# Half of an output projection as one pair group with two Strassen steps, its last eight K tiles taken token half by token half

## The chip, the cores and the metric

One core of a Trainium2 chip runs the whole program. The metric is device time in microseconds (us) of one execution; the median of several runs stands for a kernel. The engines are named as the profile names them: PE multiplies matrices, DVE and ACT work element by element, POOL does little here, SP issues the loads, and DMA engines move the data.

## The reference, cut to what matters

The program is one layer of an encoder over 256 tokens of width 2048, in float32. The change is in the first feed-forward block, just before the first layer norm:

```python
D_MODEL, SEQ, D_FF = 2048, 256, 5504

def swiglu_ffn(x, w_in, w_out):
    g, u = jnp.split(x @ w_in, 2, axis=-1)
    return (jax.nn.silu(g) * u) @ w_out

h = x
h = layer_norm(ALPHA * h + 0.5 * swiglu_ffn(h, ffn1_w_in[l], ffn1_w_out[l]), ln_ffn1_g[l], ln_ffn1_b[l])
mix = hybrid_mixer(h, w_in[l], gate_bias[l], rel_bias[l], q_a_norm[l], w_q_b[l], kv_a_norm[l],
                   w_kv_b[l], w_o_a[l], w_o_b[l], w_out[l], cos, sin)
```

The mixer's first product in the kernel is `h @ w_va` (a part of `w_in`). A second, equal feed-forward block (`ffn2`) ends the layer.

## The kernel before, in words

**Arithmetic.** Every float32 operand is split into a high part (rounded to the fast matmul format, by ACT) and a low part (the rest, by DVE). A product takes three matmuls: high by high, high by low, low by high. A *K tile* is 128 rows of the contraction; a matmul multiplies one K tile of 128 tokens with 512 columns of weights. The 256 tokens are two *token halves* (`tt` 0 and 1), whose residual rows are the tiles `h0` and `h1`.

**Weights.** `run` walks a list of items; each names the weight pieces it needs. `fetch` loads a piece (128x2048, 1 MB) into one of three `raw` tiles over SP's queue, ACT casts it into a high tile and DVE subtracts for the low tile (`halves`). High and low go to a pair of the pools `hi`/`lo` (two pairs), or to named blocks (`T0` to `T3`, `X0` to `X3`, `H0` to `H5`) where the item gives tags. The tile framework puts each engine's instructions in one fixed order by priorities and its own estimate of readiness; on the chip each engine works through its order and waits where an input is missing.

**Pair groups.** `pair_group` computes 1024 columns for both token halves in four PSUM tiles (bank of 512 columns each), two K tiles to a step: a plain step is `mm_pair`, 24 matmuls. A step in `at` goes through Strassen's scheme (`mm_sums`): the 2x2 block product of two K tiles and two column halves takes seven block products in place of eight, 21 matmuls. Its price: `weight_sums` forms four sums of weight blocks on DVE, these are cast and subtracted as well, four sums of the activations ("forms", `forms_step`) must exist, and four more PSUM tiles are filled, which `shared` combines once per group (two ACT copies, four DVE operations) before `then` adds the results to `h0` and `h1`.

**The place of the change.** The hidden width (43 K tiles) is worked in two parts, 24 and 19 K tiles. For the second part of `ffn1` the hidden tiles are the blocks `H0` to `H4` (four K tiles in each, three in `H4`). Columns 0 to 1023 are a pair group with Strassen steps 3, 5 and 7 (`out_pair`). Columns 1024 to 2047 (quarters n = 2 and 3 of 512 columns) are done by `out_proj`: quarter 2 in five pieces of four K tiles (the last has three), each for both token halves; of quarter 3 the first piece likewise; its last four pieces go through `skewed`, which runs token half 0 through all four and then token half 1 through the same weights, kept in the `T` and `X` blocks. Every finished PSUM tile is added to `h0` or `h1` (`finish`), and `ln_piece` takes statistics of the quarter.

**The hand-over to the layer norm.** `skewed` weaves the norm of token half 0 into the work of token half 1: `ln_scale` (aggregate the statistics, nine small DVE operations for the reciprocal root `y` and the offset `nb`), then `ln_T`: scale a quarter of `h0` (DVE and ACT alternately), transpose it on PE, apply gain and bias on the way out of PSUM (ACT and DVE alternately, 128 columns each), and split it into the tiles `T0` to `T3`. The next product, `h @ w_va`, starts with token half 0 and reads `T0` first.

Of the kernel before, what the change touches and what calls it, by code (L numbers as in the profile page):

```python
# [28 lines left out]
AT_FIRST = 4, 6  # L29
SUMS_OUT = ({3: ("X1", 0), 5: ("X1", 1), 7: ("X0", 0), 9: ("X0", 1)},  # L30
            {3: ("X1", 0), 5: ("X1", 1), 7: ("X0", 0)})
SUMS_GATE, AT_GATE = {**SUMS_IN, 5: ("F", 0)}, ((2, 4, 5, 6), (2, 4, 5, 6), (2, 4, 6), (2, 4, 6))
ORDER_GATE = (0, 2, 1, 4, 5, 3, 6, 7)
SUMS_YB = {4: ("T0", 0), 6: ("T0", 1), 2: None}
# [67 lines left out]
class Kernel:  # L102
# [451 lines left out]
    def ffn(self, tag, xT, st, first=None, steps=None, late=None, before=None, tags=None):  # L554


        t = self.t
        f0 = bank = 0
        turn = None
        fx = {}  # L560
        for half, nf in enumerate(F_SPLIT):
            hid, fh, homes = Act([]), {}, SUMS_OUT[half]
            end = half == len(F_SPLIT) - 1
            form = lambda c, fh=fh, homes=homes, hid=hid: self.forms_step(fh, homes, c, lambda: hid)
            for g in range(-(-nf // 4)):
# [12 lines left out]
                if turn and n < 4:  # L578
                    turn[5] = turn.pop(6)
                self.weave(main, turn or {}, prio=0)  # L580
                for c, (home, _) in homes.items():
                    if home == "X1" and c // 2 == g - 1:
                        self.add(form(c))
                hidden, turn = self.hidden(ps, bank, g, n, hid, qs)
                self.add(hidden, prio=SOON)
                if before and 2 <= j < 6:
                    self.add(lambda q=j - 2: self.gb_apply(2, self.h, (q,)), prio=LATE)
                if j == 0 and first is not None:
                    for c in set(SUMS_IN) - set(AT_FIRST):
                        self.add(self.forms_step(fx, SUMS_IN, c, xT, False))  # L590
                bank ^= 1
            if end and late:
                self.add(lambda: setattr(self, "cut", True))

            def out(hid=hid):
                x = lambda: hid
                src = [t[tag + "_w_out"][g, :, f0 * 1024:(f0 + nf) * 1024] for g in range(2)]
                self.out_pair(bank, src[0], 0, nf, x, homes, fh, half == 0, st if end else None,
                              SUM_HOME + ("H5",) if end else SUM_HOME)
                if end:  # L600
                    self.out_proj(tag + "_w_out_r", nf, x, False, st, steps, tags, 2, cut=tags is None)
# [41 lines left out]
    def group_tiles(self, j):  # L643
        return {(tt, g): self.group_tile(j) for tt in range(2) for g in range(2)}

    def pair_group(self, bank, src, n, nk, x, at, fx, ps, qs, then=None, sums_in=SUM_HOME, order=None):


        order = range(-(-nk // 2)) if order is None else order
        sums = [c for c in order if c in at]  # L650
        for i, c in enumerate(order):
            kts = range(2 * c, min(2 * c + 2, nk))
            ap = src[:, kts[0] * 2 * n:(kts[-1] + 1) * 2 * n]
            if c in at:
                close = i + 1 < len(order) and order[i + 1] in at

                def fn(w, c=c, close=close):
                    if c == sums[0]:
                        qs.update((a, self.group_tile(bank + 1)) for a in range(4))
                    self.mm_sums(ps, qs, w, n, x(), fx[c], 2 * c, c == sums[0], c == sums[-1], close)  # L660
                self.add(fn, Sums(ap, *sums_in))
                if c == sums[-1]:
                    self.add(lambda: self.shared(qs, n), prio=SOON)
                    if then:
                        self.add(then)
                continue

            def fn(w, i=i, kts=kts):
                if i == 0:
                    ps.update(self.group_tiles(bank))  # L670
                self.mm_pair(ps, w, n, x(), kts, i == 0, i == len(order) - 1)
            self.add(fn, ap)

    def shared(self, qs, n):
# [85 lines left out]
    def out_proj(self, wname, nk, x, scale, st, steps=None, tags=None, n0=0, other=False, cut=False):  # L760
# [48 lines left out]
                part(n, (0, 1), i, ps)  # L809
        if steps is not None:  # L810
            self.skewed(lambda tt, j, **kw: part(3, (tt,), last + j, ps, **kw), steps(0), tags)

    def skewed(self, part, steps, tags=None):

# [874 lines left out]
def _halves(w):  # L1689

    w = w.reshape(w.shape[0], -1, 2, 512)
    return [w[:, :, i].reshape(w.shape[0], -1) for i in (0, 1)]


def _cols(v):
    return v.reshape(-1, P).T


def _layout(i):
# [8 lines left out]
    for f in ("ffn1", "ffn2"):  # L1708
        w = a[f + "_w_in"][0]
        r[f + "_w_in"] = _pairs(  # L1710
            w[:, D_FF:D_FF + NG * 512], w[:, :NG * 512], 512, [AT_FIRST] + [SUMS_IN] * (NG - 1))
        r[f + "_w_in_r"] = _pairs(
            w[:, D_FF + NG * 512:], w[:, NG * 512:D_FF], D_FF - NG * 512, [SUMS_IN])
        w = a[f + "_w_out"][0]
        at = [*SUMS_OUT[0], *(F_SPLIT[0] // 2 + c for c in SUMS_OUT[1])]
        r[f + "_w_out"] = _pairs(*_halves(w), 512, [at, at])
        r[f + "_w_out_r"] = _tok(w[F_SPLIT[0] * P:, D // 2:])
    r["ffn2_gate"] = _tok(a["ffn2_w_in"][0][:, :512])
    r["ffn2_up"] = _tok(a["ffn2_w_in"][0][:, D_FF:D_FF + 512])
    w = a["w_in"][0]  # L1720
# [56 lines left out]
```

## Time and profile before

| what | us |
|---|---|
| median of 3 runs | 2434.72 (2433.43 to 2435.46) |
| the profiled execution | 2432.52 |
| its span in the profile | 2430.7 |
| PE busy | 2422.3 |
| DVE busy | 2130.9 |
| ACT busy | 1553.2 |
| the 19 K tiles of columns 1024 to 2047, first to last matmul of it | 630.5 to 683.4 |

The profile names a line by its number in this kernel and a tile by the program's name without its buffer number. "A<-B,C" means that A is written from B and C. A timeline row gives start, length, engine, line, operation, tiles, shape and count, and in brackets how long the engine was idle before it and who ended the wait. Busy PE time is modelled, since matmuls are pipelined: one matmul is given as about 0.39 us, but the next starts 0.227 us later.

### The profile page before, as it was taken

Reading aid. Unit: us, or ns where it says so; the run is one execution under the profiler, and the core shown is the slowest. Engines: PE = TensorE matmul, PEld = TensorE weight load, DVE = VectorE, ACT = ScalarE, POOL = GpSimd, SP = SyncE. Lnnn points to the kernel's source line nnn. Section 1 sums busy time; section 2 is a strip of 40 time slices with the busy share of each in tenths; the row PEclk is TensorE's granted clock in tenths of the full one; section 3 lists DMA queues with packets and bytes.
Section 4 is the critical chain, followed back from the end, with each engine's and each line's share of the span. In section 5 each row is a group of like instructions: output and inputs, shape, how many; then the busy total and the mean of one; then the engine's idle time right before and its main releaser. Section 6 shows DMA issues by size and latency. Waiting matters only on the chain.

```text
span 2430.7 us, 29702 instructions
## 1 busy us (share of the span) xinstructions
PE 2422.3 (100%) x11280; PEld 2022.8 (83%) x11280; DVE 2130.9 (88%) x2437; ACT 1553.2 (64%) x2022; POOL 35.9 (1%) x81
## 2 busy tenths in 40 slices
PE   9999999999999999999999999999999999999999
PEld 8888888888888888888888888888888888888887
DVE  8999989899889998779788889979879999888997
ACT  6676745666555557878565687765666675556662
POOL 0000000000000001000000000000000000000000
PEclk9999999999999999999999999999999999999999
DMA  7766656667656657776577577655556766666665
GB/s 268 252 212 214 207 200 222 210 201 219 224 176 215 216 195 248 229 210 176 183 246 256 167 241 213 220 181 192 190 199 214 229 221 210 220 207 207 200 220 182
DMA packets 176414, 516.20 MB, mean 212 GB/s; under 512 B 111728, under 2 KB 112496, under 8 KB 121104
## 3 DMA queue, kind: packets, MB, share of 16 engines
q1 hardware_dynamic: 170816, 495.83, 61.6%
q0 software_dynamic: 4592, 17.30, 2.2%
q8 instruction: 88, 1.44, 0.2%
q10 hardware_dynamic: 864, 1.18, 0.1%
q14 instruction: 54, 0.44, 0.1%
HBM read 485.30 MB, written 2.10 MB: 201 GB/s over the span
## 4 chain that ended last, share of the span: by engine, by line
PE 89%; DVE 4%; ACT 3%; DMA 1%; issue 1%; SPq 0%; DVEq 0%; ACTq 0%
PE at L311 24%; PE mm L311 23%; PE at L366 11%; PE mm L366 11%; PE mm L298 10%; PE mm L277 4%; PE mm L279 2%; DVE lo L267 2%; ACT hi L264 1%; PE at L1034 1%; PE at L1505 0%; PE at L277 0%; DMA raw<-w_xv 0%; PE at L1088 0%; ACT H L854 0%
## 5 line engine op out<-in xcount | busy, mean ns | idle before, releaser
L264 ACT CAST hi<-raw 128x1024 fp32r<-128x1024 f32 (+1 forms) x852 | 804.0, 981 | 458.0 <-PE at L311 150.1
L267 DVE TENSOR_TENSOR lo<-raw,hi 128x2048 fp32r<-128x2048 f32 (+1 forms) x427 | 902.0, 2114 | 134.8 <-ACT hi L264 129.0
L311 PE MATMUL mm<-hi,T 128*128 128x512 f32 (+1 forms) x1312 | 307.5, 384 | 0.8 <-DVE v L400 0.7
L311 PEld LDWEIGHTS mm<-hi,T 128*128 128x128 f32 x1312 | 244.5, 188 | 46.9 <-DVE v L400 1.1
L264 ACT CAST X<-H 128x1024 fp32r<-128x1024 f32 (+1 forms) x170 | 174.8, 1035 | 160.9 <-DVE H L248 119.9
L311 PE MATMUL at<-hi,T 128*128 128x512 f32 x1136 | 272.3, 390 | 0.0
L311 PEld LDWEIGHTS at<-hi,T 128*128 128x128 f32 x1136 | 213.3, 188 | 44.5
L267 DVE TENSOR_TENSOR X<-H,X 128x2048 fp32r<-128x2048 f32 (+1 forms) x85 | 191.4, 2252 | 64.7 <-ACT X L264 64.7
L311 PE MATMUL mm<-lo,T 128*128 128x512 f32 (+1 forms) x656 | 158.4, 383 | 0.0
L311 PE MATMUL at<-lo,T 128*128 128x512 f32 x568 | 141.0, 389 | 0.0
L311 PEld LDWEIGHTS mm<-lo,T 128*128 128x128 f32 x656 | 122.3, 188 | 22.4
L311 PE MATMUL at<-hi,H 128*128 128x512 f32 x560 | 133.8, 390 | 0.0
L311 PEld LDWEIGHTS at<-lo,T 128*128 128x128 f32 x568 | 106.7, 188 | 22.1
L311 PEld LDWEIGHTS at<-hi,H 128*128 128x128 f32 x560 | 105.0, 188 | 21.5
L250 DVE TENSOR_TENSOR H<-H,raw 128x512 f32<-128x512 f32 (+1 forms) x170 | 115.4, 679 | 2.2
L311 PE MATMUL mm<-hi,H 128*128 128x512 f32 x480 | 115.5, 392 | 0.1
L311 PEld LDWEIGHTS mm<-hi,H 128*128 128x128 f32 x480 | 89.6, 188 | 18.9 <-DVE w L684 0.5
L248 DVE TENSOR_TENSOR H<-raw 128x1024 f32<-128x1024 f32 (+1 forms) x85 | 102.1, 1201 | 0.6 <-DMA raw<-w_gate 0.4
L366 PE MATMUL mm<-X,X 128*128 128x512 f32 x342 | 91.4, 393 | 0.0
L264 ACT CAST X<-raw 128x1024 fp32r<-128x1024 f32 (+1 forms) x54 | 55.4, 1035 | 47.9 <-DVE raw L250 38.6
L366 PE MATMUL at<-X,X 128*128 128x512 f32 (+1 forms) x315 | 82.6, 386 | 0.7 <-ACT X L264 0.7
L854 ACT COPY w<-w 128x1024 uint16<-128x1024 uint16 (+1 forms) x60 | 75.7, 1275 | 1.4 <-DMA w<-w 1.4
(387 smaller groups left out, 4151.3 us busy)
## 6 DMA issues: line engine op xcount, KB each, us to landing
raw<-ffn_w_in SPq DMA_DIRECT2D x150, 1024.0 KB, 4.9
raw<-ffn_w_out SPq DMA_DIRECT2D x66, 1024.0 KB, 4.9
raw<-w_gate SPq DMA_DIRECT2D x32, 1024.0 KB, 4.8
raw<-ffn_w_out_r SPq DMA_DIRECT2D x16, 1024.0 KB, 4.9
raw<-w_qk SPq DMA_DIRECT2D x16, 1024.0 KB, 5.6
raw<-w_o_b SPq DMA_DIRECT2D x16, 1024.0 KB, 4.8
raw<-w_out SPq DMA_DIRECT2D x16, 1024.0 KB, 5.0
raw<-w_xk SPq DMA_DIRECT2D x16, 1024.0 KB, 5.4
```

Source lines behind the costliest of these rows:

```text
L248: self.nc.vector.tensor_tensor(two[0], two[1], raw[:, :m].unsqueeze(1).to_broadcast([P, 2, m]), ALU.add)
L250: self.nc.vector.tensor_tensor(t[:, a * m:a * m + m], t[:, b * m:b * m + m], raw[:, a * m:a * m + m], ALU.add)
L264: self.last_hi = self.nc.scalar.copy(hi[:, c:d], src[:, c:d])
L267: self.last_lo = self.nc.vector.tensor_tensor(lo[:, :n], src, hi[:, :n].bitcast(F32), ALU.subtract)
L277: self.nc.tensor.matmul(ps, hi[j], x.both(kt), start=(j == 0), stop=False)
L279: self.last_mm = self.nc.tensor.matmul(ps[:, :S], lo[j], x.at(0, kt), start=False, stop=(j == n - 1))
L298: self.last_mm = self.nc.tensor.matmul(ps, x.at(xi, kt)[:, tt * P:(tt + 1) * P], w[wi][:, j * 512 + c:j * 512 + c + m], start=(start and j ...
L311: self.last_mm = self.nc.tensor.matmul(ps[tt, g][:, :n], x.at(xi, kt)[:, tt * P:(tt + 1) * P], w[wi][:, c:c + n], start=first and j + wi + ...
L366: self.last_mm = self.nc.tensor.matmul(bank[:, :m], a[xi], v[wi][:, c * m:(c + 1) * m], start=own and first and wi + xi == 0, stop=own and ...
L854: self.nc.scalar.copy(self.words(u, n).rearrange("p (c k) -> p k c", k=2), self.words(s, n).rearrange("p (k c) -> p k c", k=2))
L1034: nc.tensor.matmul(ps[:, c0:c0 + nk], q[:, tt * P:(tt + 1) * P], k[:, :nk], start=(j == 0), stop=(j == len(parts) - 1))
```

## The change

For `ffn1` alone, columns 1024 to 2047 of the second part become one pair group over all four PSUM tiles, left open at its end (`open_end`), followed by `skewed`:

- The pair group takes the steps 6, 3, 8, 5, 7, 9 (two K tiles each, step 9 only K tile 18). Steps 3 and 5 go through Strassen's scheme, with the activation sums that the first 1024 columns used already (block `X1`), and weight sums in `H5`, `X2` and `X3`.
- The remaining eight K tiles (0 to 5, 8 and 9) are four pieces of 128x2048: for quarter 2 two pieces, for quarter 3 two. Token half 0 takes all four, then token half 1 the same four. Each of the four PSUM tiles is finished when its second piece is done.
- The weights are laid out anew to fit. The loads keep their number (ten) and bytes (9.5 MB).

`ffn2` keeps `out_proj`. The diff, cut to its core:

```diff
+AT_OUT, OUT_ORDER, OUT_ENDS = (3, 5), (6, 3, 8, 5, 7, 9), (0, 1, 2, 3, 4, 5, 8, 9)
...
-                if end:
+                if end and tags:
+                    self.out_skew(bank ^ 1, src[1], tag + "_w_out_r", nf, OUT_ORDER, OUT_ENDS, x,
+                                  {c: homes[c] for c in AT_OUT}, fh, False, st, steps, tags, SUM_HOME + ("H5",))
+                elif end:
                     self.out_proj(tag + "_w_out_r", nf, x, False, st, steps, tags, 2, cut=tags is None)
...
-                self.mm_pair(ps, w, n, x(), kts, i == 0, i == len(order) - 1)
+                self.mm_pair(ps, w, n, x(), kts, i == 0, not open_end and i == len(order) - 1)
...
+    def out_skew(self, bank, src, wname, nk, order, ends, x, at, fx, scale, st, steps, tags=None, sums_in=SUM_HOME):
+        nc, t, h = self.nc, self.t, self.h
+        ps, qs, kept = {}, {}, {}
+        def shared():
+            for (tt, a), s in qs["add"].items():
+                hs = h[tt][:, (2 + a) * 512:(3 + a) * 512]
...
+                    nc.vector.tensor_tensor(hs, hs, s, ALU.add)
+        def part(tt, j, tags=None, held=0, keep=False, again=False):
+            a, i = divmod(j, 2)
+            grp = ends[4 * i:4 * i + 4]
+            def fn(w=None):
+                if keep:
+                    kept[j] = w
+                w = kept.pop(j) if again else w
+                n, p = 2 + a, ps[tt, a]
+                self.mm_tok(p, tt, w, x(), grp, False, i == 1)
+                if i:
+                    with self.prio(SOON):
+                        self.finish(tt, n, p, False, st)
+            ap = t[wname][a, :, 2048 * i:2048 * i + 2048]
+            self.add(fn, *(() if again else ((ap, tags),)), held=held)
+        self.pair_group(bank, src, 512, nk, x, at, fx, ps, qs, shared, sums_in, order, True)
+        self.skewed(part, steps(0), tags)
```

Outside this stage every engine keeps its order. Three places inside it are shown; a number in a name marks the one buffer.

On DVE, at the end of the stage, before: the last steps for the root `y`, the offset `nb`, the scaling of `h0`, the first four pieces out of PSUM, the low half of `T0`, and then the last sum of token half 1 (`mm_756`).

```order
L379 TENSOR_SCALAR y_765_5091<-a_766_5092,y_765_5091 128x1
L403 SCALAR_TENSOR_TENSOR nb_767_5094<-mv_763_5089,y_765_5091 128x1
L413 TENSOR_SCALAR h0_101<-h0_101,mv_763_5089,y_765_5091 128x512 x2
L430 TENSOR_SCALAR w2_773_5150<-at_772_5145,vecs_89 128x128
L430 TENSOR_SCALAR w2_775_5163<-at_774_5158,vecs_89 128x128
L430 TENSOR_SCALAR w2_773_5150<-at_772_5145,vecs_89 128x128
L430 TENSOR_SCALAR w2_775_5163<-at_774_5158,vecs_89 128x128
L256 TENSOR_TENSOR T0_768_5140<-w2_773_5150,T0_768_5140 128x4x128
L754 TENSOR_TENSOR h1_102<-h1_102,mm_756_5015 128x512
```

The same place with the change (lines count one to four higher; `mm_732` is token half 1 of quarter 3, the last PSUM tile of the stage):

```order
L379 TENSOR_SCALAR a_780_5116<-y_779_5115,v_778_5114 128x1
L758 TENSOR_TENSOR h1_102<-h1_102,mm_732_4831 128x512
L380 TENSOR_SCALAR y_779_5115<-a_780_5116,y_779_5115 128x1
L391 BN_STATS bn_728_4824<-h1_102 128x6
L379 TENSOR_SCALAR a_780_5116<-y_779_5115,v_778_5114 128x1
L396 BN_AGGR mv_794_5236<-bn_728_4824 128x2
L380 TENSOR_SCALAR y_779_5115<-a_780_5116,y_779_5115 128x1
L401 TENSOR_SCALAR v_795_5237<-mv_794_5236 128x1
L404 SCALAR_TENSOR_TENSOR nb_781_5118<-mv_777_5113,y_779_5115 128x1
L414 TENSOR_SCALAR h0_101<-h0_101,mv_777_5113,y_779_5115 128x512 x2
```

The sum of the stage's last PSUM tile has moved from behind `T0` to a place ahead of `nb`, the scaling of `h0` and `T0`.

On PE, the transposes of `h0` (tiles `at`) and the first product of `w_va`, before:

```order
L298 MATMUL mm_756_5015<-X1_748_4962,H3_655_4336 128x512 x4
L421 MATMUL at_772_5145<-ident_90,h0_101 128x128 x4
L421 MATMUL at_774_5158<-ident_90,h0_101 128x128 x4
L298 MATMUL mm_756_5015<-X2_750_4968,H4_707_4680 128x512 x6
L298 MATMUL mm_756_5015<-X3_751_4969,H4_707_4680 128x512 x3
L421 MATMUL at_776_5182<-ident_90,h0_101 128x128 x4
L421 MATMUL at_778_5195<-ident_90,h0_101 128x128 x4
L298 MATMUL mm_788_5229<-hi_753_4997,T0_768_5140 128x512 x8
```

With the change:

```order
L299 MATMUL mm_732_4831<-X3_767_5000,H1_561_3742 128x512 x2
L299 MATMUL mm_732_4831<-X3_767_5000,H2_610_4055 128x512 x2
L422 MATMUL at_786_5171<-ident_90,h0_101 128x128 x4
L422 MATMUL at_788_5184<-ident_90,h0_101 128x128 x2
L422 MATMUL at_790_5211<-ident_90,h0_101 128x128
L422 MATMUL at_788_5184<-ident_90,h0_101 128x128
L422 MATMUL at_790_5211<-ident_90,h0_101 128x128
L422 MATMUL at_788_5184<-ident_90,h0_101 128x128
L422 MATMUL at_790_5211<-ident_90,h0_101 128x128 x2
L422 MATMUL at_792_5224<-ident_90,h0_101 128x128 x4
L299 MATMUL mm_802_5258<-hi_769_5030,T0_782_5166 128x512 x8
```

All 16 transposes now stand behind the last matmul of token half 1, where the first eight stood nine matmuls ahead of it; the first matmul of `w_va` follows them at once, as before.

On ACT, from the scaling of `h0` to the high half of `T0`, before:

```order
L415 ACTIVATE h0_101<-h0_101,nb_767_5094,y_765_5091 128x512 x2
L428 ACTIVATE w2_773_5150<-at_772_5145,vecs_89 128x128
L428 ACTIVATE w2_775_5163<-at_774_5158,vecs_89 128x128
L428 ACTIVATE w2_773_5150<-at_772_5145,vecs_89 128x128
L428 ACTIVATE w2_775_5163<-at_774_5158,vecs_89 128x128
L255 CAST T0_768_5140<-w2_773_5150 128x4x128
```

With the change:

```order
L416 ACTIVATE h0_101<-h0_101,nb_781_5118,y_779_5115 128x512 x2
L429 ACTIVATE w2_787_5176<-at_786_5171,vecs_89 128x128
L429 ACTIVATE w2_789_5189<-at_788_5184,vecs_89 128x128
L429 ACTIVATE w2_791_5216<-at_790_5211,vecs_89 128x128
L429 ACTIVATE w2_787_5176<-at_786_5171,vecs_89 128x128
L429 ACTIVATE w2_789_5189<-at_788_5184,vecs_89 128x128
L429 ACTIVATE w2_791_5216<-at_790_5211,vecs_89 128x128
L429 ACTIVATE w2_793_5229<-at_792_5224,vecs_89 128x128
L256 CAST T0_782_5166<-w2_787_5176 128x4x128
```

Seven pieces out of PSUM stand ahead of the cast of `T0`, where there were four.

More of the change, by code (lines that the diff above doesn't have):

```diff
@@ L644, in group_tiles, with pair_group @@
         return {(tt, g): self.group_tile(j) for tt in range(2) for g in range(2)}
-    def pair_group(self, bank, src, n, nk, x, at, fx, ps, qs, then=None, sums_in=SUM_HOME, order=None):
+    def pair_group(self, bank, src, n, nk, x, at, fx, ps, qs, then=None, sums_in=SUM_HOME, order=None, open_end=False):
         order = range(-(-nk // 2)) if order is None else order
@@ L811, in out_proj @@
             self.skewed(lambda tt, j, **kw: part(3, (tt,), last + j, ps, **kw), steps(0), tags)
+    def out_skew(self, bank, src, wname, nk, order, ends, x, at, fx, scale, st, steps, tags=None, sums_in=SUM_HOME):
[4 more added lines that the diff above has]
+                hs = h[tt][:, (2 + a) * 512:(3 + a) * 512]
+                if scale:
+                    nc.vector.scalar_tensor_tensor(hs, hs, ALPHA, s, ALU.mult, ALU.add)
+                else:
+                    nc.vector.tensor_tensor(hs, hs, s, ALU.add)
[15 more added lines that the diff above has]
+        self.skewed(part, steps(0), tags)
     def skewed(self, part, steps, tags=None):
@@ L1692, in _halves, with _tiles @@
     return [w[:, :, i].reshape(w.shape[0], -1) for i in (0, 1)]
+def _tiles(w, kts):
+    import numpy as np
+    return np.concatenate([w[k * P:k * P + P] for k in kts])
 def _cols(v):
@@ L1715, in _layout @@
         at = [*SUMS_OUT[0], *(F_SPLIT[0] // 2 + c for c in SUMS_OUT[1])]
-        r[f + "_w_out"] = _pairs(*_halves(w), 512, [at, at])
-        r[f + "_w_out_r"] = _tok(w[F_SPLIT[0] * P:, D // 2:])
+        skew = f == "ffn1"
+        at2 = [*SUMS_OUT[0], *(F_SPLIT[0] // 2 + c for c in AT_OUT)] if skew else at
+        r[f + "_w_out"] = _pairs(*_halves(w), 512, [at, at2])
+        w = w[F_SPLIT[0] * P:, D // 2:]
+        r[f + "_w_out_r"] = _tok(_tiles(w, OUT_ENDS) if skew else w)
     r["ffn2_gate"] = _tok(a["ffn2_w_in"][0][:, :512])
```

## The prediction

> **What bounds the kernel now.** I read the page first, then the timelines of PE, DVE and ACT around 620 to 700 us, then a table by stretches.
>
> ```profile
> PE 2422.3 (100%) x11280; PEld 2022.8 (83%) x11280; DVE 2130.9 (88%) x2437; ACT 1553.2 (64%) x2022; POOL 35.9 (1%) x81
> PE 89%; DVE 4%; ACT 3%; DMA 1%; issue 1%; SPq 0%; DVEq 0%; ACTq 0%
> core 0: us, PE busy (x) PEld busy (x) DVE busy (x) ACT busy (x) POOL busy (x), PEclk, DMA share, GB/s
> 628.30:680.10 51.80, 51.80 (x230) 42.74 (x228) 39.33 (x40) 23.40 (x25) 0.00 (x0) 1.00 0.72 248
> ```
>
> PE is busy for the whole span and carries 89% of the chain of waits. So a matmul less saves its interval, and any new idle time of PE is added in full, since nothing later on PE can give it back. In the stretch that is changed DVE works 39.3 of 51.8 us. Now PE there, by start and length:
>
> ```profile
> 630.49 1.98 PE L298 MATMUL mm<-hi,H 128*128 128x512 f32 x8
> 667.21 4.92 PE L298 MATMUL mm<-X,H 128*128 128x512 f32 x21
> 671.97 5.60 PE L298 MATMUL mm<-T,H 128*128 128x512 f32 x24
> 677.41 2.88 PE L298 MATMUL mm<-X,H 128*128 128x512 f32 x12
> 680.27 1.06 PE L421 MATMUL at<-ident,h 128*128 128x128 f32 x8
> 681.09 2.32 PE L298 MATMUL mm<-X,H 128*128 128x512 f32 x9
> 683.25 1.03 PE L421 MATMUL at<-ident,h 128*128 128x128 f32 x8
> 684.04 2.28 PE L298 MATMUL mm<-hi,T 128*128 128x512 f32 x8
> ```
>
> 21 matmuls from 667.21 to 671.97 are 0.2267 us each. PE is without a gap but for 677.41 + 12 x 0.2267 = 680.13 to 680.27. What hides the layer norm of token half 0 is token half 1: from 671.97 on, PE has 36 matmuls before the first transposes and nine more before the rest. DVE and ACT meanwhile:
>
> ```profile
> 628.34 2.29 DVE L267 TENSOR_TENSOR lo<-raw,hi 128x2048 fp32r<-128x2048 f32 x1
> 674.40 0.69 DVE L390 BATCH_NORM_STATS2 bn<-h 128x6 f32<-128x512 f32 x1
> 677.20 0.26 DVE L395 BATCH_NORM_AGGREGATE mv<-bn 128x2 f32<-128x24 f32 x1
> 679.55 0.16 DVE L403 SCALAR_TENSOR_TENSOR nb<-mv,y 128x1 f32<-128x1 f32 x1
> 679.63 1.00 DVE L413 TENSOR_SCALAR h<-h,mv,y 128x512 f32<-128x512 f32 x2
> 683.68 0.69 DVE L256 TENSOR_TENSOR T<-w,T 128x512 fp32r<-128x512 f32 x1 [0.34 <-ACT T L255]
> 684.29 0.68 DVE L754 TENSOR_TENSOR h<-h,mm 128x512 f32<-128x512 f32 x1
> 679.75 1.52 ACT L415 ACTIVATE h<-h,nb,y 128x512 f32<-128x512 f32 x2 [4.88 <-DVE nb L403]
> 681.17 1.73 ACT L428 ACTIVATE w<-at,vecs 128x128 f32<-128x128 f32 x4
> 683.03 1.14 ACT L255 CAST T<-w 128x512 fp32r<-128x512 f32 x2
> ```
>
> The low half of `T0` starts at 683.68 and PE takes up `w_va` at 684.04; only at 684.29 does DVE add the last sum of token half 1. That order is what the change turns round.
>
> **Matmuls.** Before, 19 K tiles x 2 token halves x 2 quarters x 3 passes = 228. Now two steps of 24 become 21: 222. Saved: 6 x 0.2267 = 1.36 us. From 630.49 the last one is issued out at 630.49 + 222 x 0.2267 = 680.8.
>
> **DVE's added work** in the stage, by the costs of one operation:
>
> ```profile
> L267 DVE TENSOR_TENSOR lo<-raw,hi 128x2048 fp32r<-128x2048 f32 x16 | 36.5, 2287 | 7.7 <-ACT hi L264 7.7
> L267 DVE TENSOR_TENSOR lo<-raw,hi 128x1024 fp32r<-128x1024 f32 x1 | 1.2, 1220 | 0.0
> L250 DVE TENSOR_TENSOR H<-H,raw 128x512 f32<-128x512 f32 x6 | 4.1, 686 | 0.0
> L248 DVE TENSOR_TENSOR H<-raw 128x1024 f32<-128x1024 f32 x3 | 3.7, 1218 | 0.0
> L631 DVE TENSOR_TENSOR h<-h,w 128x512 f32<-128x512 f32 x4 | 2.6, 685 | 0.0
> L681 DVE TENSOR_TENSOR w<-w,mm 128x512 f32<-128x512 f32 x1 | 0.7, 681 | 0.0
> ```
>
> Weight sums, 2 x (1.22 + 2 x 0.69) = 5.2; low parts, one more 2048 and one 1024, 2.29 + 1.22 = 3.5; four operations of `shared` and four sums into `h`, 8 x 0.68 = 5.5. Together 14.2, and about 13 with the 0.08 by which queued operations overlap (16 of them). ACT gets three more casts of 1024 (1.0 each, the second row below) and two copies beside 23.4 us of work in 51.8, so ACT has room. DVE up to the last sum of token half 1: 39.3, less the norm chain from 677.20 (2.9), plus 13, plus the aggregation and five small operations of the root, which now stand ahead of that sum (1.3) = 50.7, of the 52.5 us from 628.34 to 680.8. So DVE, which before waited 12.5 us in this stretch, can wait less than 2 now before it comes late. What it waits for are casts, and they for loads:
>
> ```profile
> raw<-ffn_w_out_r SPq DMA_DIRECT2D x16, 1024.0 KB, 4.9
> 655.98 2.00 ACT L264 CAST T<-raw 128x1024 fp32r<-128x1024 f32 x2 [2.03 <-DMA raw<-ffn_w_out_r]
> ```
>
> Number, bytes and queue of the loads stay, but a load is issued when DVE frees a `raw` tile, so a late DVE also makes late loads. `X1`, `X2` and `X3` serve the Strassen steps until step 5 is through and can be refilled only then, some 50 matmuls (11 us) before PE reads `X1` and `X2`; casts of 2.0 and a subtraction of 2.3 must fit in there, and a load of 4.9 where its `raw` tile comes free late. I take 0.5 us of lateness, bounds 0 and 2.
>
> **First stall, at the hand-over.** The sum of `mm_732` stands on DVE ahead of the rest of `h0`'s root. It waits for the stage's very last matmul; behind it wait `nb`, the scaling of `h0`, so the transposes, so `T0`, so all of PE. From PE's last matmul: how soon does DVE take up such a sum?
>
> ```profile
> 2416.09 5.04 PE L298 MATMUL mm<-X,H 128*128 128x512 f32 x30
> 2421.17 0.42 DVE L787 TENSOR_TENSOR h<-h,mm 128x256 f32<-128x256 f32 x1
> ```
>
> 0.04 after the modelled end, and that end is 0.39 - 0.23 = 0.16 behind the interval: 0.2. Then the sum 0.6 and the statistics 0.6 (0.68 and 0.69 less overlap), six small operations at 0.16 (the `nb` row) to 0.24 (677.20 to 679.63 over ten), so 1.0 to 1.45, half of the scaling row 0.5, and 0.1 until PE starts. Together 3.0 to 3.5; I take 3.25.
>
> **Second stall.** The 16 transposes take about 1.65 (681.09 - 680.27 is 0.82 for eight); they existed before and cost nothing new. But `w_va` needs `T0`: from `nb`, ACT scales two quarters (681.17 - 679.75 = 1.4), then seven pieces at 1.73 / 4 = 0.43 make 3.0, then the cast 0.6: 5.0. PE, from `nb`: 0.65 to the transposes, 1.65 for them, 2.3. It waits 2.7. One matmul later it needs the low half, 0.69 behind the cast: 0.5 more. So 3.2; with pieces at 0.35 it is 2.6, with DVE late on its own seven pieces 3.7.
>
> **Sum.** -1.36 (matmuls) - 0.14 (the gap at 680.13) + 0.5 + 3.25 + 3.2 = +5.45 us. Nothing hides it: PE has no other work queued there. The norm of token half 1 gains: its statistics are now taken earlier, and its transposes come after 36 matmuls (8 us), as before. The profiled execution (2432.52) becomes 2438.0, the median of the runs (2434.72), which lies 2.2 above it, 2440.2. The ends are -1.5 + 0 + 3.0 + 2.6 = +4.1 and -1.5 + 2 + 3.5 + 3.7 = +7.7: 2438.8 to 2442.4.
>
> **Rivals.** First, **PE's clock falls** in the hand-over, and the next matmuls run slowly. The rows on it:
>
> ```profile
> 1.06 4.21 PE L493 MATMUL at<-w 128*128 128x128 f32 x18 [1.06 <-DVE w L470]
> 5.04 4.84 PE L311 MATMUL mm<-hi,T 128*128 128x512 f32 x16
> 2425.26 1.02 PE L1617 MATMUL mm<-T,w 128*128 128x512 f32 x2
> 2427.00:2429.00 2.00, 0.00 (x0) 0.00 (x0) 0.66 (x2) 0.00 (x0) 0.00 (x0) 1.00 0.97 349
> 2429.00:2430.70 1.70, 0.00 (x0) 0.00 (x0) 0.00 (x0) 0.00 (x0) 0.00 (x0) 0.52 0.16 52
> ```
>
> PE's last matmul ends at 2426.28; the granted clock (the figure ahead of the DMA share) is 1.00 until 2429.0 and 0.52 behind: it halved after some 2.8 us without work. The stalls here are about 3.2 and 3.2 us with 1.65 of transposes between them. At half clock a matmul takes 0.23 longer; at the program's start, with work from 1.06 on, the 16 from 5.04 still took 4.84 - 0.16 = 4.68, 1.05 more than 16 x 0.2267, part of it perhaps waiting for data. So a fall costs between 1.05 and half of some 5 us, 2.5; I take 1.8: 2442.0. Against it: transposes are work too, and no row shows how little suffices. The Trainium skill ("TensorE: Matmul & The Clock Gate", Part 1 and Part 4) has a free-running window of about 3.4 us, half clock after an idle one, and says that transposes don't count as busy in the same way; the end of this trace agrees with the first, no run here shows the second. By that rule alone an estimate would be 1.7 us for each cold window.
>
> Second, **the hand-over is short**, the case on the other side. If pieces leave PSUM at 0.35 or faster, DVE is never late and the small operations take 0.16, the terms are 0, 3.0 and 2.6: +4.1, 2438.8, which can't be told from no change. It decides from 6.4 us of stalls downwards. For it: PE's stalls are paced by short operations whose waits overlap. Against it: DVE's room of 1 to 2 us.
>
> Third, **only the matmuls count**: the hand-over is hidden as before, and the time is 2434.72 - 1.36 = 2433.4. For it: before, PE waited nowhere here. Against it stands the order on DVE. The six matmuls themselves are gone by count, so the saving is not in doubt.
>
> Fourth, **the group starves**: `X1` to `X3` come late and PE waits inside the group, 2 us or more on top: 2442.2 and higher.
>
> **Chances.** Forecast 0.47, falling clock 0.24, short hand-over 0.20, matmuls only 0.03, starved group 0.06. 0.2% (4.9 us, about what a measurement of this kernel tells from no change) is at 2439.6, so some 0.1 of the forecast's 0.47 counts as no change. Slower: 0.37 + 0.24 + 0.06 = 0.67; within 0.2%: 0.10 + 0.20 + 0.02 = 0.32; faster 0.01. The range must take in the short hand-over and the falling clock: 2437.3 to 2443.8.
>
> **What would show it.** In the changed profile: 222 matmuls in the stage; PE idle about 3.2 us ahead of the first transposes of `h0`, put down to DVE, and 2.5 to 3.5 more ahead of the first `w_va` matmuls, put down to ACT and DVE; DVE's sum of `mm_732` within 1 us of PE's last matmul. A lower clock would show in a table of stretches behind it. I am wrong if PE goes through the hand-over with less than 4 us of idle time, if it waits over 2 us inside the group, or if the time moves elsewhere.

## The result, and the profile after

| | us |
|---|---|
| median before | 2434.72 (2433.43 to 2435.72, 7 runs) |
| median after | 2441.22 (2440.6 to 2443.9, 7 runs) |
| ratio | 1.0032, 95% interval 1.0022 to 1.0041 |
| predicted | 2440.2 (2437.3 to 2443.8) |

The changed kernel is slower by 6.5 us. Its profiled execution is the longest of the seven (2443.9), so its hand-over may be longer than in most; four more profiles of the same program stand further down. The first rows of its page, engines and chain of waits:

```profile
PE 2426.6 (99%) x11274; PEld 2023.1 (83%) x11274; DVE 2144.3 (88%) x2453; ACT 1557.0 (64%) x2027; POOL 36.0 (1%) x81
PE 88%; DVE 5%; ACT 3%; DMA 2%; issue 2%; SPq 0%; DVEq 0%; ACTq 0%
```

PE has six matmuls less (11274 for 11280) and is yet busy 4.3 us longer: some of its work ran more slowly. PE at the hand-over, from the timeline (start, length, engine, line, operation, tiles, count; in brackets the idle time before and who ended it):

```profile
630.36 3.79 PE L312 MATMUL mm<-hi,H 128*128 128x512 f32 x16
676.13 5.60 PE L299 MATMUL mm<-X,H 128*128 128x512 f32 x24
685.25 2.98 PE L422 MATMUL at<-ident,h 128*128 128x128 f32 x16 [3.52 <-issue]
689.82 4.11 PE L299 MATMUL mm<-hi,T 128*128 128x512 f32 x8 [1.59 <-ACT T L256]
693.73 1.91 PE L299 MATMUL mm<-lo,T 128*128 128x512 f32 x4
701.30 1.04 PE L422 MATMUL at<-ident,h 128*128 128x128 f32 x8
```

The last matmul is issued out at 676.13 + 24 x 0.2267 = 681.57; from there to the transposes 3.68 us pass. The 16 transposes take 2.98, where before eight took 0.82 from start to next start. After 1.59 of idle time the first eight matmuls of `w_va` take 3.9, against 2.1 before (684.04 to 686.15). DVE and ACT in the same place:

```profile
679.68 0.14 DVE L376 TENSOR_SCALAR y<-v 128x1 int32<-128x1 int32 x1
679.73 2.28 DVE L268 TENSOR_TENSOR H<-raw,H 128x2048 fp32r<-128x2048 f32 x1
681.93 0.27 DVE L379 TENSOR_SCALAR a<-y,v 128x1 f32<-128x1 f32 x1
682.67 0.68 DVE L758 TENSOR_TENSOR h<-h,mm 128x512 f32<-128x512 f32 x1
683.39 0.69 DVE L391 BATCH_NORM_STATS2 bn<-h 128x6 f32<-128x512 f32 x1
684.53 0.16 DVE L404 SCALAR_TENSOR_TENSOR nb<-mv,y 128x1 f32<-128x1 f32 x1
684.61 1.00 DVE L414 TENSOR_SCALAR h<-h,mv,y 128x512 f32<-128x512 f32 x2
684.73 1.52 ACT L416 ACTIVATE h<-h,nb,y 128x512 f32<-128x512 f32 x2 [6.76 <-DVE nb L404]
689.14 1.67 ACT L256 CAST T<-w 128x512 fp32r<-128x512 f32 x3
```

DVE has no idle time here: behind the first step of the root (679.68) stands the low half of a `w_va` weight (679.73). DVE comes out of this split at 681.9, then works through the rest of the root, and the sum of `mm_732` (682.67) and its statistics (683.39) stand inside that root. Only then come `nb` and the scaling. In the kernel before, such a split was done ahead of the whole root, which began at 677.20:

```profile
675.01 2.27 DVE L267 TENSOR_TENSOR H<-raw,H 128x2048 fp32r<-128x2048 f32 x1
```

The table of stretches shows the clock (stretch; busy time of PE, PEld, DVE, ACT, POOL with instructions; granted clock of PE; DMA share; GB/s), cut where the record of the clock can change:

```profile
682.57:685.98 3.41, 0.72 (x7) 0.76 (x8) 3.37 (x13) 1.25 (x2) 0.00 (x0) 1.00 0.83 298
685.98:689.39 3.41, 2.25 (x12) 1.85 (x9) 2.92 (x11) 3.02 (x9) 0.00 (x0) 0.50 0.04 14
689.39:692.81 3.42, 2.99 (x6) 2.11 (x7) 3.42 (x10) 3.42 (x7) 0.00 (x0) 0.50 0.00 0
692.81:696.22 3.41, 3.41 (x9) 2.64 (x8) 2.13 (x3) 2.16 (x3) 0.00 (x0) 0.50 0.00 0
696.22:699.63 3.41, 3.41 (x16) 2.77 (x15) 1.07 (x1) 0.00 (x0) 0.00 (x0) 1.00 0.40 84
```

For three stretches of 3.41 us, 10.24 us, PE ran at half clock. As **stage length** I use from here on the time from the stage's first matmul (630.36) to the transposes of token half 1 in `w_va` (701.30): 70.94 us, against 692.52 - 630.49 = 62.03 before. So 8.9 of the 11.4 us by which this execution's span is longer lie here. The rest comes in small pieces from 1300 us on (matched matmul by matmul, PE is 8.8 us later than before at 1000 us, 8.3 at 1300 and 10.8 at its last matmul) and behind the last matmul (0.6); nothing of the change is there, and no single piece on PE is over 0.5 us.

### The profile page after: what moved, and what is told of

Read it like the earlier page. It is cut to its first block, busy times and chain, and to the rows that moved or that the text cites. A ratio compares the mean times of both kernels' runs of the same rounds, so it can differ in the third digit from the quotient of the medians.

```text
span 2442.1 us, 29713 instructions
## 1 busy us (share of the span) xinstructions
PE 2426.6 (99%) x11274; PEld 2023.1 (83%) x11274; DVE 2144.3 (88%) x2453; ACT 1557.0 (64%) x2027; POOL 36.0 (1%) x81
## 4 chain that ended last, share of the span: by engine, by line
PE 88%; DVE 5%; ACT 3%; DMA 2%; issue 2%; SPq 0%; DVEq 0%; ACTq 0%
PE at L312 24%; PE mm L312 22%; PE at L367 11%; PE mm L367 10%; PE mm L299 9%; PE mm L278 5%; PE mm L280 2%; DVE lo L268 2%; ACT hi L265 2%; PE at L1073 1%; DMA raw<-w_xq 1%; PE at L1544 0%; PE at L1127 0%; DVE raw L251 0%; PE at L278 0%
## 5 line engine op out<-in xcount | busy, mean ns | idle before, releaser
L312 PE MATMUL mm<-hi,H 128*128 128x512 f32 x536 | 129.7, 391 | 0.3 <-DVE w L688 0.3
L312 PEld LDWEIGHTS mm<-hi,H 128*128 128x128 f32 x536 | 100.1, 188 | 21.5 <-DVE w L688 0.8
L367 PE MATMUL at<-X,X 128*128 128x512 f32 (+1 forms) x333 | 87.9, 387 | 1.2 <-ACT X L265 1.0
L367 PEld LDWEIGHTS mm<-X,X 128*128 128x128 f32 x342 | 63.4, 188 | 15.4 <-DVE X L268 2.2
```

What stands on the lines that cost most here:

```text
L312: self.last_mm = self.nc.tensor.matmul(ps[tt, g][:, :n], x.at(xi, kt)[:, tt * P:(tt + 1) * P], w[wi][:, c:c + n], start=first and j + wi + ...
L367: self.last_mm = self.nc.tensor.matmul(bank[:, :m], a[xi], v[wi][:, c * m:(c + 1) * m], start=own and first and wi + xi == 0, stop=own and ...
```

## The experiments

Three causes were set against each other: the **order** of DVE's work at the hand-over, PE's **clock** behind it, and the two **Strassen steps** by themselves (DVE's sums and low parts, late loads). The kernel before ran on the same chip: median 2433.34 us (31 runs) beside the first four kernels, 2433.61 us (23 runs) beside the three that follow and the changed kernel itself.

### The sum behind the norm

```diff
-                    with self.prio(SOON):
+                    with self.prio(SOON), self.tc.issue_after(self.chain.ins) if tt else nullcontext():
                         self.finish(tt, n, p, False, st)
```

The finishing sums of token half 1 are issued behind `nb` of `h0`; everything else stays as changed.

> Kernel after, but DVE's sums of token half 1 (quarters 2 and 3) are issued behind the offset nb of token half 0's norm; every load, matmul and DVE operation stays, and PE's order stays. Theory 'order': in the kernel after, the sum of the last PSUM tile waits for PE's last matmul and holds the rest of the norm. Ahead of it DVE is free for the norm at 681.9 us, so the scaling of h0 could come at about 683.3 in place of 684.6; the wait of PE ahead of the transposes falls from 3.7 to about 2.2 us, and the time from 2441.2 to about 2439 or, if the clock then stays up, 2437. Theory 'load': DVE's added work makes the norm late whatever the order; the wait stays within 0.5 us of 3.7 and the time within 1 us of 2441.2.

Measured 2438.98 us (2435.29 to 2441.25, 9 runs), ratio to before 1.0021 (1.0012 to 1.0031). PE in its timeline:

```profile
675.55 5.60 PE L299 MATMUL mm<-X,H 128*128 128x512 f32 x24
682.36 1.06 PE L422 MATMUL at<-ident,h 128*128 128x128 f32 x8 [1.21 <-issue]
684.44 1.09 PE L422 MATMUL at<-ident,h 128*128 128x128 f32 x8 [1.01 <-DVE h L414]
686.15 0.50 PE L299 MATMUL mm<-hi,T 128*128 128x512 f32 x1 [0.62 <-ACT T L256]
686.88 3.28 PE L299 MATMUL mm<-hi,T 128*128 128x512 f32 x7 [0.23 <-DVE y L376]
```

The gap ahead of the transposes falls to 682.36 - 680.99 = 1.37, from 3.68 here and 3.07 to 3.68 in the five profiles shown below: the two sums of token half 1 and what came with them made 1.7 to 2.3 us of the first stall (1.5 was expected). What is left stands on DVE ahead of the first scaling: the weight split, still ahead of the root's last step, and the first of the two sums.

```profile
678.60 2.28 DVE L268 TENSOR_TENSOR H<-raw,H 128x2048 fp32r<-128x2048 f32 x1
681.12 0.68 DVE L758 TENSOR_TENSOR h<-h,mm 128x512 f32<-128x512 f32 x1
```

A new wait of 1.0 arises between the transposes, since the second sum (682.78) now stands between the two scalings. Stage length 66.18. The clock was half for one stretch only (from 686.5), and the seven matmuls at 686.88 ran in it.

### No Strassen steps, or one

```diff
-AT_OUT, OUT_ORDER, OUT_ENDS = (3, 5), (6, 3, 8, 5, 7, 9), (0, 1, 2, 3, 4, 5, 8, 9)
+AT_OUT, OUT_ORDER, OUT_ENDS = (), (6, 3, 8, 5, 7, 9), (0, 1, 2, 3, 4, 5, 8, 9)
```

> Kernel after with all six steps of the pair group plain (no weight sums, six matmuls more, as many as before); group order and the eight K tiles token half by token half stay. Theory 'order and load': without the Strassen steps DVE has some 13 us less to do, the framework puts h0's norm and the first transposes ahead of the last sum again, PE waits under 1 us at the hand-over, the clock stays full: 2434.7 to 2435.7. Rival 'the new ending': eight K tiles, 48 matmuls, four tiles finished at the end are too little cover for the norm; PE still waits over 3 us and the time stays over 2438.

Measured 2434.77 us (2433.5 to 2437.33, 11 runs), ratio 1.0007 (0.9998 to 1.0016). With 228 matmuls again, the pair group and the token halves alone cost nothing that can be told: the scheduler put the first eight transposes back among token half 1's matmuls, and the stage is 62.45 long. With one step:

```diff
-AT_OUT, OUT_ORDER, OUT_ENDS = (3, 5), (6, 3, 8, 5, 7, 9), (0, 1, 2, 3, 4, 5, 8, 9)
+AT_OUT, OUT_ORDER, OUT_ENDS = (3,), (6, 8, 5, 3, 7, 9), (0, 1, 2, 3, 4, 5, 8, 9)
```

> Kernel after with one Strassen step in place of two (K tiles 6 and 7), taken as the fourth step (order 6, 8, 5, 3, 7, 9); step 5 is plain. Three matmuls fewer than before. Theory 'order': DVE has half of the added work, the framework puts h0's norm ahead of the last sum, PE waits under 1 us: 2434.7 - 0.7 + 0 to 0.8 = 2434.0 to 2434.8. Theory 'any Strassen step here costs more than its matmuls': 2436 or more.

Measured 2433.49 us (2431.51 to 2435.07, 11 runs), ratio 1.0000 (0.9991 to 1.0009), stage 61.91, no stretch at half clock. Three matmuls (0.7 us) are saved, which is below what can be told. Both kernels take Strassen work away, but both also have another order at the hand-over; these two runs alone don't separate the causes.

### PE kept busy in the gaps

```diff
+FILL = 14, 10
...
+        def fill(n):
+            def fn():
+                p = self.at_tile()
+                with self.tc.issue_after((self.last_turn if n == FILL[1] else self.last_mm).ins):
+                    for _ in range(n):
+                        self.last_mm = nc.tensor.matmul(p, x().at(0, 13)[:, :P], self.fill_w[:, :512], start=True, stop=True)
+            return fn
...
+        side = {0: begin, 4: [fill(FILL[0]), *quarters[0], *quarters[1], fill(FILL[1])]}
```

14 matmuls more stand ahead of `h0`'s transposes and ten behind them. They read a hidden tile and old weights and write a PSUM tile that nobody reads. The order on DVE also shifts a little towards the norm.

> Kernel after with 24 matmuls that nothing reads put into PE's idle time: 14 between the last matmul of token half 1 and the transposes of h0, 10 between the transposes and the first product of w_va. Theory 'clock': the fall to half clock for 10.2 us in the profiled execution came of the idle time; with PE kept busy the granted clock stays 1.00 in every stretch there, the 16 transposes and the first products take the time they took before, and the time is 2434.7 - 1.4 + 24 x 0.2267 + 0 to 1.2 = 2438.7 to 2440.0, with a smaller spread, although PE has more to do. Rival 'the clock costs nothing here' (PE would wait for T0 anyway): the time is as after, 2441.2 or, if the filling delays the norm, more.

Measured 2438.22 us (2437.72 to 2439.09, 11 runs), ratio 1.0020 (1.0011 to 1.0029). PE:

```profile
681.02 3.34 PE L858 MATMUL at<-X,H 128*128 128x512 f32 x14
684.20 1.95 PE L423 MATMUL at<-ident,h 128*128 128x128 f32 x16
686.97 2.56 PE L858 MATMUL at<-X,H 128*128 128x512 f32 x10 [0.82 <-DVE w L432]
689.37 1.98 PE L300 MATMUL mm<-hi,T 128*128 128x512 f32 x8
```

The time is 0.5 us below the range expected. The clock stays at 1.00 through the stage: the transposes take 1.95, the eight matmuls of `w_va` 1.8 from start to next start, and the stage is 67.24. With 24 x 0.2267 = 5.4 us of useless work PE comes out sooner than in every profile of the changed kernel (68.35 to 70.94), and the runs spread over 1.4 us only. From the first matmul of `w_va` to the next transposes it takes 697.53 - 689.37 = 8.16, where the five profiles of the changed kernel take 9.94 to 11.48 with PE at half clock in part of it. So part of the loss is the clock. How much exactly this run can't say, as DVE's order moved as well (`nb` comes 2.4 us behind the last matmul of token half 1, for 3.0).

### The order alone, in the kernel before

```diff
+        if behind:
+            scale = steps[0][0]
+            def begin():
+                with self.tc.issue_after(self.last_sum.ins):
+                    scale()
+            steps = [begin], steps[1], steps[2]
-        self.weave(main, dict(zip((0, 3, 4), steps)))
+        self.weave(main, {4: [f for s in steps for f in s]} if behind else dict(zip((0, 3, 4), steps)))
```

> The kernel before, with its work unchanged (no pair group, no Strassen step in columns 1024 to 2047), but with the layer norm of token half 0 ordered on DVE behind the last sum of token half 1, and so all 16 transposes behind the stage's last matmul. If the order alone makes the hand-over's cost (theory), PE waits some 4 us ahead of the first transposes (one sum, one scaling, and the root's whole chain of some ten small operations of 0.16 to 0.25 us, since all of it now comes behind) and 1.5 to 3 us ahead of w_va; with no lower clock 6 to 8 us more than before, 2440 to 2442 us, with the clock at half for one to three stretches of 3.41 us up to 3 us more. If the Strassen steps' own work on DVE (weight sums, low parts, late loads) makes the cost (rival), this kernel has none of it and stays within 2 us of before.

Measured 2440.35 us (2439.76 to 2442.2, 5 runs), ratio 1.0032 (1.002 to 1.0045): the loss of the change, with no Strassen step and no new loads. PE and DVE:

```profile
677.04 4.92 PE L298 MATMUL mm<-X,H 128*128 128x512 f32 x21
686.29 1.08 PE L421 MATMUL at<-ident,h 128*128 128x128 f32 x4 [4.33 <-issue]
682.00 0.69 DVE L754 TENSOR_TENSOR h<-h,mm 128x512 f32<-128x512 f32 x1 [6.41 <-PE mm L298]
685.65 0.99 DVE L413 TENSOR_SCALAR h<-h,mv,y 128x512 f32<-128x512 f32 x2
```

Here DVE waits for the stage's last matmul, as the prediction had it, and takes the sum 0.2 us behind it (677.04 + 21 x 0.2267 = 681.80). The stage is 70.22, with one stretch at half clock (from 686.31). So the order is enough to make a loss of this size. The rival (Strassen steps) expected no more than 2 us. The shares are not the same as in the changed kernel: here the whole root stands behind the sum, not its last steps, and the first stall is 686.29 - 681.80 = 4.49 for 3.07 to 3.68.

### Both Strassen steps, with the order mended

```diff
-        self.skewed(part, steps(0), tags)
+        for j in range(4):
+            part(0, j, tags=tags[j], held=UNITS, keep=True)
+        main = self.collect(lambda: [part(1, j, again=True) for j in range(4)])
+        begin, *quarters = steps(0)
+        for f in begin:
+            self.add(f, prio=SOON, held=UNITS)
+        self.weave(main, dict(zip((3, 4), quarters)))
```

`held` keeps the splits of the next weights behind the work that is due first.

> The changed kernel with both Strassen steps, all 222 matmuls and the same loads; only the order is mended: the splits of the w_va weights are held back behind h0's offset, and the quarters of the norm are woven into token half 1 again, so that eight transposes stand 11 matmuls ahead of its end. By the order theory, with the durations of the changed kernel's trace, PE waits some 0.6 us ahead of the transposes and 2.1 + 0.6 ahead of w_va, less 1.5 for the matmuls: 1.5 to 2.5 us more than before (2436 to 2437), and no stretch at half clock, since no wait is over 2.2 us. If the two Strassen steps cost by themselves (rival), it stays at 2440 to 2441.

Measured 2437.26 us (2435.16 to 2439.96, 11 runs), ratio 1.0016 (1.0007 to 1.0025). From PE's timeline and the table of stretches:

```profile
679.47 1.06 PE L422 MATMUL at<-ident,h 128*128 128x128 f32 x8 [0.97 <-issue]
685.89 0.49 PE L299 MATMUL mm<-hi,T 128*128 128x512 f32 x1 [1.95 <-ACT T L256]
686.75 2.81 PE L299 MATMUL mm<-hi,T 128*128 128x512 f32 x7 [0.37 <-DVE T L257]
684.02:687.43 3.41, 1.17 (x4) 0.77 (x5) 3.41 (x7) 1.50 (x3) 0.00 (x0) 1.00 0.98 375
687.43:690.85 3.42, 3.42 (x10) 2.65 (x9) 3.35 (x14) 3.15 (x5) 0.00 (x0) 0.50 0.42 177
```

The waits are about those expected (1.1 for 0.6, 2.1, 0.6); that no stretch would be at half clock was wrong. Waits of 2.1 and 0.6 us behind eight transposes were enough, where they fell into one stretch. The clock did not fall in every run: averaged over the execution and rounded to three digits it is 0.999 in seven of the eleven runs (mean time 2438.0) and 1.000 in four (2436.2), which suggests some 1.8 us for one stretch at half clock with the work and the order unchanged. Stage 66.43. The last kernel of this kind also sets the pair group's steps to 6, 8, 3, 7, 5, 9:

> As the run before, and the pair group's steps in the order 6, 8, 3, 7, 5, 9, so that the two Strassen steps stand apart and DVE has a plain step between them. Order theory: about 1.6 + 0.5 us of waiting ahead of w_va, less 1.5 for the matmuls, 0 to 1.5 us more than before (2434 to 2436), so it can't be told from before. Rival (Strassen steps cost by themselves): 2440 to 2441. If DVE can't be freed by order because it is full (third theory: DVE is the bound of this stage with two Strassen steps), it is over 2437.

Measured 2435.29 us (2432.94 to 2436.59, 11 runs), ratio 1.0006 (0.9997 to 1.0015): both Strassen steps, all 222 matmuls, and no difference from before that can be told.

```profile
677.73 1.03 PE L422 MATMUL at<-ident,h 128*128 128x128 f32 x8
678.52 2.99 PE L299 MATMUL mm<-X,H 128*128 128x512 f32 x12
683.72 0.49 PE L299 MATMUL mm<-hi,T 128*128 128x512 f32 x1 [1.34 <-ACT T L256]
```

PE goes from token half 1 into the transposes without a gap, and waits only ahead of `w_va` (1.34, and 0.37 at the next matmul, by the rows). Stage 62.58, clock 1.00. This speaks against the two other theories: by themselves the Strassen steps cost nothing that can be told, and DVE isn't too full to serve them. The 1.36 us saved and 0.55 more (62.58 for 62.03) go into the wait ahead of `w_va`. The profile is of one of the shorter executions (2433.53); the clock, averaged in the same way, is 0.999 in five of the eleven, against one of 23 before, so some may still have a stretch at half clock, which no trace shows.

### The changed kernel four times more

The first profile had three stretches at half clock. The changed kernel ran again, unedited, to see whether that is fixed by the work:

> The changed kernel once more, beside the others on one chip. If the clock's fall differs from execution to execution, this profile may show one, two or three stretches of 3.41 us at half clock behind the hand-over, the idle time itself stays at 3.5 to 3.8 and 1.5 to 3.3 us, and the times spread over 2 to 3 us (2440 to 2444). If the fall is fixed by the order of the work, the profile shows 10.2 us at half clock again and the hand-over costs 8.8 to 9 us again.

> The changed kernel, one more profile (this and the next two runs are looks at one question: why do its hand-overs cost 8.9 and 6.5 us in two profiles of one program?). Theory: the granted clock is set anew every 3.41 us on a grid that runs freely against the program; a stretch with over 60% idle on PE makes the next one half, and only a stretch that is about 90% busy brings the full clock back. With L the end of the last matmul of token half 1 and b the first grid point behind L: b from 0 to 0.7 us gives three half stretches, about 0.7 two, 1.0 three, over 2 none or one; without a half stretch the stage up to the next transposes is 66 to 67 us long (62.0 before), and each half stretch adds up to 1.7. Rival: the fall is fixed by the work, then the number is two or three whatever b is.

> As the run before: the number of half stretches of 3.41 us and their start on the grid (start of the full clock plus whole multiples of 3.4133 us), the stage 66 to 67 us long without one and up to 1.7 us longer for each. Rival: always two or three.

> As the two before. If all three show two or three half stretches with b spread over the 3.41 us, the grid does not decide and the rival holds.

The first of these gave 2440.14 us (2438.0 to 2442.16, 7 runs), ratio 1.0027 (1.0016 to 1.0038); the others, one execution each, 2440.32, 2441.98 and 2441.72 (the kernel before, one execution beside them, 2436.01). PE in the second profile, whose stage starts at 631.21 and has the middle length of the five:

```profile
676.50 5.60 PE L299 MATMUL mm<-X,H 128*128 128x512 f32 x24
685.28 2.88 PE L422 MATMUL at<-ident,h 128*128 128x128 f32 x16 [3.18 <-issue]
689.76 3.73 PE L299 MATMUL mm<-hi,T 128*128 128x512 f32 x8 [1.60 <-ACT T L256]
699.70 1.03 PE L422 MATMUL at<-ident,h 128*128 128x128 f32 x8
```

The five profiles, all in us. "Late" is the last matmul's end less the stage's start less 222 x 0.2267; "first stall" runs from there to the transposes; the next column from the first transpose to the first matmul of `w_va`; the next from that to the transposes of token half 1 (8.48 before); b is the distance from the last matmul's end to the next point of the clock's grid, the points 3.413 us apart at which the granted clock can change.

| profile | late | first stall | transposes to `w_va` | `w_va` part | stage | b | at half clock |
|---|---|---|---|---|---|---|---|
| first | 0.88 | 3.68 | 4.57 | 11.48 | 70.94 | 0.99 | 10.24 |
| second | 0.40 | 3.34 | 4.48 | 9.94 | 68.49 | 0.75 | 6.83 |
| third | 0.46 | 3.07 | 4.08 | 10.44 | 68.38 | 2.09 | 3.41 |
| fourth | 0.53 | 3.07 | 4.22 | 10.20 | 68.35 | 0.77 | 6.83 |
| fifth | 0.53 | 3.59 | 5.25 | 10.40 | 70.10 | 0.12 | 3.41 + 3.41 |

Each stretch at half clock starts a whole multiple of 3.413 us behind the first start of the full clock (the first one 199 times, in the third profile 201 times), and that start differs from execution to execution (4.2 to 7.0 us from the program's start in these profiles). One, two and three stretches occur, so the fall is not fixed by the work. The rule in the expectations was made from the first two profiles. It holds for the third (b over 2: one) and the fourth (b near 0.7: two), not for the fifth: two stretches in place of three, with a full one between them. The table of stretches of the third and then of the fifth profile:

```profile
683.47:686.88 3.41, 1.94 (x16) 1.73 (x16) 3.27 (x14) 2.95 (x7) 0.00 (x0) 1.00 0.51 214
686.88:690.30 3.42, 1.51 (x5) 1.05 (x6) 3.42 (x11) 3.42 (x9) 0.00 (x0) 1.00 0.00 0
690.30:693.70 3.40, 3.40 (x9) 2.64 (x8) 2.14 (x5) 3.38 (x5) 0.00 (x0) 0.50 0.00 0
```

```profile
681.44:684.85 3.41, 0.04 (x1) 0.00 (x0) 3.34 (x14) 0.47 (x1) 0.00 (x0) 1.00 0.77 279
684.85:688.27 3.42, 3.37 (x16) 3.28 (x16) 2.31 (x9) 2.47 (x6) 0.00 (x0) 0.50 0.24 96
688.27:691.68 3.41, 1.49 (x6) 0.86 (x5) 3.41 (x11) 3.41 (x9) 0.00 (x0) 1.00 0.00 0
691.68:695.09 3.41, 3.41 (x9) 2.67 (x8) 2.36 (x5) 3.41 (x5) 0.00 (x0) 0.50 0.00 0
```

In the third profile the 16 transposes fill 57% of a stretch, and the clock stays; in the next PE is busy 44%, and the one after is half. In the fifth the idle stretch is followed by one that the transposes alone fill, and it brings the full clock back, only for the wait ahead of `w_va` to take it away again.

## Why the prediction was right or wrong

- **Sign and size** were right: 2440.2 forecast, 2441.22 measured, inside the range, and slower. The number is nearer than its working deserves, as the next points show.
- **Matmuls, -1.36**: confirmed by count, 222 in the stage.
- **DVE's lateness, 0.5**: 0.40 to 0.88 in the five profiles. PE lost it in pieces of 0.1 to 0.3 inside the group, and that DVE was their cause is not shown; the starved group did not come (no wait over 1 us inside it).
- **First stall, 3.25**: 3.07 to 3.68, right in size. Its cause was only half right. The prediction let DVE wait for the stage's last matmul with the sum of `mm_732`, and take it up 0.2 us later. In the profile DVE never waited: it was still in the root, behind the split of a `w_va` weight, and took the sum at 682.67: 1.1 behind the last matmul by its interval, 0.94 behind its modelled end (681.73), so at the edge of the 1 us that I had named. That a split could stand inside the root is in no term of the sum. With the sums of token half 1 behind `nb` 1.37 of 3.68 remain. The profile also puts this idle time down to "issue", not to DVE as I had written.
- **Second stall, 2.7 + 0.5**: transposes and wait together were to take 1.65 + 2.7 = 4.35; measured 4.08 to 5.25. The longest (4.48 to 5.25) have transposes at half clock, which lengthen them by 0.9 to 1.6 and shorten the wait behind them, as ACT and DVE work on meanwhile. PE's idle time there is 1.59 to 2.14 by the rows, under the 2.5 to 3.5 that I had named as a sign.
- **The clock**: this is the step that failed. I gave the falling clock 0.24 and held the case without it for the likeliest; it fell in all five profiles, and the granted clock averaged over the execution was 0.998 or 0.999 in all 17 executions of the changed kernel, where the kernel before has 1.000 in 54 of the 55 beside the experiments. Its price was set at 1.8. In the `w_va` part, 8.48 + 0.5 was forecast and 9.94 to 11.48 measured: 1.0 to 2.5 more, so the price was about right. What failed was the weight given to the argument against the fall, that transposes are work too and no row shows how little suffices. Transposes are work for the clock (last section), but a row of the prediction did show something of how little suffices, and I misread it. The prediction took the end of its trace to agree with a fall behind an idle stretch. But the stretch ahead of that fall (2425.66 to 2429.07) was not idle: PE was busy there for 0.62 of 3.41 us, until 2426.28. So a stretch that is mostly idle can be enough, and a stall of 3.1 to 3.7 with another of 1.6 to 2.1 behind it leaves hardly a place of the grid without one. This last step is argued from the table of five profiles, not tested apart.
- **The sum**: +5.45 forecast. By the median profile the stage is 68.49 - 62.03 = +6.5, as are the medians (2441.22 - 2434.72, and 2440.14 - 2433.61): the forecast's idle time plus about 1 us of slow matmuls, between the forecast (2440.2) and its rival (2442.0). That the two agree to 0.1 is partly luck: the five stages are 6.3 to 8.9 longer than before, and the five spans 7.8 to 11.4 (the one profile of the kernel before is of an execution 2.2 below its median).
- **The other rivals**: "only the matmuls count" fell at once. "The hand-over is short" fell on its conditions: the pieces left PSUM at 0.36 to 0.44 each, the small operations took 0.14 to 0.27, and PE lost 0.40 to 0.88 inside the stage.

What stays open: how the clock's loss and the idle time share the +6.5 exactly, since filling the gaps also moved DVE's order; and which of the edits that mend the order (splits held, transposes woven in again, steps set apart) does how much, beyond 2437.26 with the first and 2435.29 with both. No kernel here beats the one before: the two with fewer matmuls that come nearest, 2433.49 and 2435.29, can't be told from it.

## What to carry to other kernels

Where PE is the bound and a norm sits between two products, the saving in matmuls is small beside the place of the norm in DVE's order: six matmuls were worth 1.36 us, and the same 222 matmuls ran 4.9 us faster (2435.29 for 2440.14) once sums and weight splits no longer stood ahead of the norm's last steps and the steps were set apart. After any change that makes DVE fuller, look at what the scheduler now puts ahead of the chain that PE waits for, and hold back the splits and sums that nobody waits for. And price a new stall on PE with its clock: behind the two stalls of the changed kernel 1.0 to 2.5 us of slow matmuls came here, and waits of 2.1 and 0.6 us already brought a stretch at half clock.

## What the runs showed of the hardware

- In the traces the granted clock of PE changes only on a grid of 3.413 us, whose start differs from execution to execution (4.2 to 7.0 us into the program in the five profiles of the changed kernel). The Trainium skill ("TensorE: Matmul & The Clock Gate", Part 1) has a free-running window of this length; the traces agree.
- One wholly idle stretch is not needed for the fall. Stretches at full clock with PE busy 0 to 52% were followed by half clock (0.72 of 3.41 us in the first profile; 1.17 in the kernel with the splits held), all but three; stretches with 57% and more never. The bound isn't sharp: in the third profile two stretches had 44%, and only the later one was followed by half clock; the two others had 46% (second profile) and 51% (splits held, steps set apart), both in the program's last microseconds.
- To come back it took a stretch that was nearly full: at 87% (2.99 of 3.42, first profile) the clock stayed half, at 89% (the kernel before with the order alone changed) and more it rose.
- Transposes count as work for it. The same page of the Trainium skill (Part 4) says of PE's transpose mode that the full clock does not engage for it; the rows call the transposes MATMUL and don't tell whether they use that mode. Here a stretch with nothing but 16 transposes, 3.37 of 3.42 us busy, was followed by the full clock (fifth profile).
